# Grouped-query attention: keys and values of all tokens first, query finishes among the attention units, output products in halves, three engines in source order

## The chip, the cores and the metric

The kernel runs as one program on one core of a Trainium2 chip. The metric is the device time of one execution in microseconds (us). The core has TensorE (matmul; PE in the profile, its weight loads PEld), VectorE (DVE), ScalarE (ACT), GpSimd (POOL) and SyncE (SP, which here issues the DMAs). They run beside each other and wait for one another through semaphores; each works through its own list of instructions in order. Matmul results go to PSUM, which this kernel uses as eight banks of 128 x 512 float32. A *granted clock* below 1 in the profile means that TensorE ran at that share of its full speed.

## The reference, cut to what matters

The program computes a gated linear attention block with a feed-forward, then two further layers on 256 latent and 256 context tokens, 1024 features each: neighbourhood attention and a feed-forward, then grouped-query attention (16 query heads, 4 key and value heads of 64 features) and a last feed-forward. The change touches the grouped-query attention, which only the latent tokens leave (`with_ctx_out` is false there):

```python
def qknorm_gqa_mixer(h_lat, h_ctx, w_qkv, q_gain, k_gain, w_o, ang_row, ang_col, with_ctx_out):
    q, k, v = project_qkv(h_lat, w_qkv, GQA_HEADS, GQA_KV_HEADS)
    qc, kc, vc = project_qkv(h_ctx, w_qkv, GQA_HEADS, GQA_KV_HEADS)
    q = axial_rope(rms_norm_2(q, q_gain), ang_row, ang_col)
    k = axial_rope(rms_norm_2(k, k_gain), ang_row, ang_col)
    kc = rms_norm_2(kc, k_gain)
    k_all = jnp.concatenate([kc, k], axis=1)
    v_all = jnp.concatenate([vc, v], axis=1)
    ...
    def block(q_b):
        s = jnp.einsum('bqhgd,bshd->bhgqs', q_b, k_all).astype(jnp.float32) * scale
        p = jax.nn.softmax(s, axis=-1).astype(v_all.dtype)
        return jnp.einsum('bhgqs,bshd->bqhgd', p, v_all)
    ...
    y_lat = jnp.moveaxis(o, 0, 1).reshape(b, s_len, GQA_HEADS * HEAD_DIM) @ w_o
```

All is float32. The result is added to the latent residual through a gate, and the last feed-forward follows.

## The kernel before

**Split numbers and weight units.** Each float32 operand of a large product is split into a rounded high part and a low remainder, and a product is three matmuls (`mm3`, L170 to L173). The weights come as a stream of units of 128 x 1024 (list `UNITS`). `wnext` (L159) takes the next unit: it issues loads about four units ahead on SP (`w_load`, five raw buffers) and converts units ahead of use (`w_split`): ACT rounds the raw unit to its high part (L154), DVE subtracts for the low part (L155). `cap[0]` says how far ahead is converted: with 3, two units beyond the one in use. Twelve buffers hold six converted units.

**Who orders the work.** A scheduler at build time orders each engine's instructions by its own estimates, with the source order as priority, and assigns buffers. Inside a `manual_schedule` region, the engines named keep the order of the source. Before, no such region covers this part.

**The section, in source order.** Token tiles 0 and 1 are latent, 2 and 3 context; `bT2` holds the inputs, transposed and split, for all four.

1. `kv_pass((2, 3))`: keys and values of the context, 16 steps of three matmuls 512 wide (`mm_h`, one feature block k of one token tile). Its four weight units are kept in `kv_units`.
2. `to_T` (L204 to L230): the latent inputs are transposed (L210, two per block, eight blocks and so eight banks), then scaled and shifted from PSUM (even blocks on DVE, L226; odd ones on ACT, L223), rounded on ACT (L228) and subtracted on DVE (L229).
3. `q_proj(0, aq)`: first half of the queries (heads 0 to 7), both latent tiles, 16 steps; beside it, one step of `back` after each, the context's `kv_finish`: square on ACT, sums and gain on DVE, inverse root on POOL (`inv_root`, L176 to L178), rounding and remainder, and `kv_T`, which transposes the keys on TensorE (L1211), high parts first.
4. `kv_steps` for the latent tiles with the kept units, 16 steps; beside it `q_finish(0, ...)` for both tiles: square, sum, inverse root, rotation (`roped`: product L1139, two half products L1144, sum L1147), rounding (L1256), remainder (L1260), and after an empty step the transposes (L1266, one bank for four heads) with their copies (L1270) to `qst`.
5. `gqa_chain`: second half of the queries, tile 0 (8 steps, beside the latent `kv_finish`), then tile 1 and `q_finish(1, ...)`, then the output product.
6. `staged`: 32 units (`gqa_unit`: 16 heads for tile 0, then for tile 1) in a software pipeline, each unit one stage behind the next: two score matmuls into a bank (L1349, L1350); row maximum on DVE (L1355), a small product on POOL; exponential on ACT (L1358); division on DVE (L1364, for some heads on ACT, L1362); four transposes (L1368); copy on ACT (L1371). After a pair of heads comes `gqa_pv`, the product with the values (L1378, 16 matmuls 64 columns wide) and its split copy. `qfill(n)` runs three steps of `gqa_chain` per unit in the first sixteen, one per unit after. The output product takes a weight unit k per step with `mm_r` (six matmuls) as soon as `og_done` has its pair of heads. For tile 0 the units k = 4 to 7 are kept in `held`, so that tile 1 can use them at the end. After each product of tile 1, one step of `attn_out(0)` goes on with the residual and norm of tile 0; then its transposes to `eT`.
7. The held products of tile 1, its gate and norm, and the last feed-forward (`tok_up`).

Of the kernel before, what the change touches and what calls it, by code (L numbers as in the profile page):

```python
# [19 lines left out]
KD = D // P  # L20
# [63 lines left out]
def net(ctx, tc, x, xt, vecs, gk_w, gk_up, gk_b, g_onorm, wst, final_norm, ctx_in, ctx_t, ada, ada_b, cvec,  # L84
# [25 lines left out]
    def bank(dt=F32):  # L110
        return ps.tile([P, 512], dt, tag="bank", bufs=8, name=nm("b"))
# [26 lines left out]
    cap = [3]  # L138
# [190 lines left out]
    def load_gates(L, v):  # L329

        for ci in range(2):
            for half in range(2):
                if (L, ci, v) in grows:
                    gates[(L, ci, v, half)] = t2([512])
                    bcast_row(gates[(L, ci, v, half)], grows[(L, ci, v)], 512 * half, 512)

    def run(gen, n=1):
        for _ in range(n):
            next(gen, None)
# [84 lines left out]
    for f in range(8):  # L424
        u = wnext(("f", "w_in"))
# [113 lines left out]
    for k in range(KD):  # L539
        u = wnext(("r", "w_in", k))  # L540
# [615 lines left out]
    def kv_steps(ac):  # L1156
        for kp in range(4):
            if 2 in ac:
                kv_units.append(wnext(("h", "gqa_qkv", 2 * kp, D)))
                u = kv_units[-1]  # L1160
            else:
                u = kv_units.pop(0)
            for j in range(2):
                k = 2 * kp + j
                for t in ac:
                    mm_h(ac[t], u, j, bT2[k], t, k == 0, k == KD - 1)
                    yield

    def kv_pass(tiles):
        ac = {t: bank() for t in tiles}  # L1170
        for _ in kv_steps(ac):
            pass
        return ac
# [56 lines left out]
    def q_proj1(ac, t):  # L1230
        for kp in range(4):
            if t == 0:
                q1_units.append(wnext(("h", "gqa_qkv", 2 * kp, 512)))
            for j in range(2):
                k = 2 * kp + j
                mm_h(ac[t], q1_units[kp], j, bT2[k], t, k == 0, k == KD - 1)
                yield
# [35 lines left out]
    def alternate(gens):  # L1273
        while gens:
            for g in list(gens):
                if next(g, "end") == "end":
                    gens.remove(g)
                yield

    def beside(front, back):  # L1280

        for _ in front:
            next(back, None)

    cap[0] = 3
    load_gates(1, 2)
    acx = kv_pass((2, 3))
    to_T(xn, bT2, 0, mod(1, 0, 1), mod(1, 0, 0))
    back = alternate([kv_finish(acx, t) for t in (2, 3)])
    aq = [bank(), bank()]  # L1290
    beside(q_proj(0, aq), back)
    run(back, 100)
    aq0 = [aq[0], t2([512])]
    A.copy(out=aq0[1], in_=aq[1])
    back = alternate([q_finish(0, aq0, t) for t in range(2)])
    acl = {t: bank() for t in (0, 1)}
    beside(kv_steps(acl), back)
    run(back, 100)
    back = alternate([kv_finish(acl, t) for t in range(2)])
    aq = [bank(), bank()]  # L1300

    def gqa_chain():

        yield from q_proj1(aq, 0)
        yield from alternate([q_proj1(aq, 1), q_finish(1, aq, 0)])
        q1_units.clear()
        yield from q_finish(1, aq, 1)
        for t, k in [(0, k) for k in range(KD)] + [(1, k) for k in range(KD // 2)]:
            if k == 0:
                oacc.append([bank() for _ in range(2)])  # L1310
            while (k, t) not in og_done:
                yield
            u = wnext(("r", "gqa_o", k))
            if k >= KD // 2:
                held.append((k, u))
            mm_r(oacc[t], u, og[k], t, k == 0, k == KD - 1)
            if t == 1:
                run(out0)
            yield
        run(out0, 9)  # L1320
        yield
        yield from to_T_steps([xn[0]], eT, 0, mod(1, 0, 4), mod(1, 0, 3))

    def attn_out(t):
# [9 lines left out]
    oacc, og_done, held = [], set(), []  # L1334
    out0 = attn_out(0)
    eT = new_T()
    chain_ = gqa_chain()
    for _ in range(11):
        run(chain_)
        run(back, 2)  # L1340
    run(back, 100)

    og = [None] * KD

# [28 lines left out]
    def gqa_pv(hp, t):  # L1373
        po = bank()
        kvh = hp // 2
        for c in range(4):
            for e in range(2):
                T.matmul(po[e * 64:(e + 1) * 64, 0:P], lhsT=vg[(c + 2) % 4][:, kvh * 64:(kvh + 1) * 64],  # L1378
                         rhs=probs[2 * hp + e][:, c, :], start=(c == 0), stop=(c == 3))
        del probs[2 * hp], probs[2 * hp + 1]  # L1380
        yield
        if t == 0:
            z = t2([2, S], F32R)
            og[hp] = (z[:, 0, :], z[:, 1, :])
        o = [z[:, t * P:(t + 1) * P] for z in og[hp]]
        A.copy(out=o[0], in_=po[:, 0:P])
        V.tensor_tensor(out=o[1], in0=po[:, 0:P], in1=o[0], op=ALU.subtract)  # L1387
        og_done.add((hp, t))

    gorder = [(h, t) for t in range(2) for h in range(16)]  # L1390

    def qfill(n):
        run(chain_, 3 if n < 16 else 1)

    def qdone(m):
        head, t = gorder[m]
# [1 line left out]

    xn = []
    staged([lambda z=z: gqa_unit(*z) for z in gorder], qfill, qdone)  # L1400
    run(chain_, 200)
    for ks in (held[:-1], held[-1:]):
        for hf in range(2):
            c = slice(hf * 512, (hf + 1) * 512)
# [2 lines left out]
            if k == KD - 1:  # L1407
                gated(lat[1], oacc[1][hf], 1, 0, 2, hf)
    xn.append(normed(lat[1]))


    load_gates(1, 5)
# [178 lines left out]
```

## Time and profile before

| | us |
|---|---|
| median of 3 runs | 1278.57 |
| lowest, highest | 1278.46, 1279.03 |
| the profiled execution, its own time | 1278.93 |
| its span | 1277.1 |
| PE busy in the span | 1251.0 (98%) |
| DVE busy | 926.6 (73%) |
| ACT busy | 684.9 (54%) |
| POOL busy | 74.7 (6%) |

Busy time is the time in which at least one instruction of the engine is shown. A matmul's row lasts longer than the distance to the next one's start, since matmuls overlap; so the work of a stretch is read from distances between starts, and idle time from rows that name what ended it (`[0.45 <-ACT t L1201]`: idle 0.45 us, ended by ACT's instruction of line 1201). A group's row in the table of groups holds line, engine, operation, output and input with their shapes, the count, then busy us and mean ns, then the idle time before.

### The profile page before, as it was taken

How to read it: one execution, taken by the hardware profiler on the slowest of the kernel's cores; microseconds unless marked ns; L12 is line 12 of the kernel's file. 1: busy time of each engine (PE TensorE's matmuls, PEld its weight loads, DVE VectorE, ACT ScalarE, POOL GpSimd, SP SyncE). 2: the span in 40 equal slices, each digit the busy share in tenths (PEclk: the TensorE clock that was granted, in tenths of full speed). 3: DMA queues.
4: the chain of work that ended last, by engine and by line, in shares of the span. 5: the costliest groups of instructions: out<-in, count | busy, mean ns of one | idle time of the engine just before them, and what ended most of it. 6: DMA issues, size and time to landing. Idle time of an engine off the chain costs nothing.

```text
span 1277.1 us, 18786 instructions
## 1 busy us (share of the span) xinstructions
PE 1251.0 (98%) x6969; PEld 1048.0 (82%) x6969; DVE 926.6 (73%) x1640; ACT 684.9 (54%) x1305; POOL 74.7 (6%) x131
## 2 busy tenths in 40 slices
PE   7999999999999999999999999999999899999997
PEld 6888889988788877789888888888887677899996
DVE  4878788797988888777877777533668887655554
ACT  6565655666548888754232122233457877644443
POOL 1000000030100000001000000000002210000000
PEclk9999999999999999999999999999999999999999
DMA  9526587887573333463656778624654234666650
GB/s 342 182 93 213 184 294 250 286 269 257 182 253 96 115 115 119 155 199 114 213 177 212 245 263 267 192 85 120 204 171 133 60 86 128 200 188 184 186 176 34
DMA packets 68796, 231.23 MB, mean 181 GB/s; under 512 B 8208, under 2 KB 9152, under 8 KB 68704
## 3 DMA queue, kind: packets, MB, share of 16 engines
q1 hardware_dynamic: 68416, 229.94, 56.1%
q8 instruction: 55, 0.90, 0.3%
q14 instruction: 37, 0.30, 0.1%
q10 hardware_dynamic: 288, 0.09, 0.0%
HBM read 228.93 MB, written 1.07 MB: 180 GB/s over the span
## 4 chain that ended last, share of the span: by engine, by line
PE 83%; DVE 8%; ACT 6%; issue 1%; DMA 1%; POOL 0%; ACTq 0%; POOLq 0%; DVEq 0%
PE b L171 25%; PE b L172 25%; PE b L173 25%; DVE wl L155 2%; PE b L1378 1%; ACT wh L154 1%; PE b L1368 1%; PE b L503 1%; PE b L210 1%; DVE a L300 1%; DVE t L300 1%; PE b L1349 1%; ACT t L854 1%; PE b L1350 0%; PE b L933 0%
## 5 line engine op out<-in xcount | busy, mean ns | idle before, releaser
L154 ACT CAST wh<-raw 128x1024 fp32r<-128x1024 f32 x310 | 322.3, 1043 | 408.2 <-PE b L172 310.6
L155 DVE TENSOR_TENSOR wl<-raw,wh 128x1024 fp32r<-128x1024 f32 x310 | 375.6, 1218 | 161.3 <-ACT wh L154 158.0
L172 PE MATMUL b<-t,wl 128*128 128x256 f32 (+1 forms) x1120 | 366.4, 327 | 0.4 <-DVE wl L155 0.4
L171 PE MATMUL b<-t,wh 128*128 128x256 f32 (+1 forms) x1120 | 366.8, 328 | 0.0
L173 PE MATMUL b<-t,wh 128*128 128x256 f32 (+1 forms) x1120 | 365.8, 327 | 0.0
L171 PE MATMUL b<-wh,t 128*128 128x512 f32 (+1 forms) x747 | 297.4, 401 | 0.5 <-ACT t L682 0.3
L172 PE MATMUL b<-wh,t 128*128 128x512 f32 (+1 forms) x747 | 295.3, 395 | 0.4 <-DVE t L610 0.2
L173 PE MATMUL b<-wl,t 128*128 128x512 f32 (+1 forms) x747 | 294.9, 395 | 0.0
L172 PEld LDWEIGHTS b<-t,wl 128*128 128x128 f32 x1120 | 211.3, 189 | 22.8 <-DVE wl L155 0.7
L171 PEld LDWEIGHTS b<-t,wh 128*128 128x128 f32 x1120 | 211.2, 189 | 22.6 <-ACT wh L154 0.3
L173 PEld LDWEIGHTS b<-t,wh 128*128 128x128 f32 x1120 | 211.0, 189 | 20.6 <-DVE t L229 0.2
L173 PEld LDWEIGHTS b<-wl,t 128*128 128x128 f32 x747 | 140.3, 188 | 33.7
L172 PEld LDWEIGHTS b<-wh,t 128*128 128x128 f32 x747 | 140.7, 188 | 32.9 <-DVE t L1387 1.5
L171 PEld LDWEIGHTS b<-wh,t 128*128 128x128 f32 x747 | 140.2, 188 | 31.7 <-ACT t L682 0.9
L300 DVE CUSTOM_DVE_ANT_0 a<-a,crow 128x1024 f32<-128x1024 f32 x96 | 117.7, 1233 | 27.7 <-DMA a<-in_ada_dram 27.4
L300 DVE CUSTOM_DVE_ANT_0 t<-a,crow 128x1024 bf16<-128x1024 f32 x64 | 78.0, 1228 | 7.3 <-DMA a<-in_ada_dram 7.2
L1041 DVE TENSOR_TENSOR t<-b,t 128x512 f32<-128x512 f32 (+1 forms) x42 | 23.7, 563 | 61.6 <-PE b L173 54.5
L183 POOL TENSOR_TENSOR c<-c,mhalf 128x1 f32<-128x1 f32 x21 | 14.2, 674 | 539.0 <-DVE c L182 538.9
L315 POOL TENSOR_TENSOR mod<-mod,bcol 128x8 f32<-128x8 f32 x20 | 15.2, 759 | 477.5 <-DVE mod L300 475.2
L1047 ACT CAST t<-t 128x512 fp32r<-128x512 f32 (+1 forms) x42 | 21.7, 517 | 23.2 <-DVE t L1041 23.1
L190 ACT ACTIVATE t<-t 128x512 f32<-128x512 f32 x40 | 24.8, 624 | 9.1 <-DVE t L1010 4.7
L1358 ACT ACTIVATE t<-b,c,c 128x512 f32<-128x512 f32 x32 | 25.2, 790 | 0.3 <-POOL c L1356 0.2
(225 smaller groups left out, 1198.5 us busy)
## 6 DMA issues: line engine op xcount, KB each, us to landing
raw<-in_wst_dram SPq DMA_DIRECT2D x310, 512.0 KB, 4.3
a<-in_ada_dram SPq DMA_DIRECT2D x96, 512.0 KB, 4.4
t<-in_rpb_dram SPq DMA_DIRECT2D x16, 256.0 KB, 4.6
t<-row SPq DMA_DIRECT2D x12, 256.0 KB, 4.6
t<-in_ctx_dram SPq DMA_DIRECT2D x8, 256.0 KB, 6.1
t<-in_xt_dram SPq DMA_DIRECT2D x4, 256.0 KB, 4.0
t<-in_x_dram SPq DMA_DIRECT2D x4, 256.0 KB
crow<-in_cvec_dram SPq DMA_DIRECT2D x2, 512.0 KB
```

Source lines behind the costliest of these rows:

```text
L154: A.copy(out=h[:, :n], in_=raw[:, :n])
L155: V.tensor_tensor(out=l[:, :n], in0=raw[:, :n], in1=h[:, :n], op=ALU.subtract)
L171: T.matmul(o, lhsT=lh, rhs=rh, start=first, stop=False)
L172: T.matmul(o, lhsT=ll, rhs=rh, start=False, stop=False)
L173: T.matmul(o, lhsT=lh, rhs=rl, start=False, stop=last)
L183: G.tensor_tensor(out=ms[:, 3:4], in0=ms[:, 2:3], in1=mhalf[:, 0:1], op=ALU.pow)
L190: A.activation(out=junk[hf], in_=halves[hf], func=AF.Square, scale=1.0 / 32.0, accum_out=ms[:, hf:hf + 1])
L300: V.tensor_tensor_reduce(out=raw if ci == n_c - 1 else t2([D], BF16), in0=raw, in1=crow[ci], scale=1.0, scalar=0.0, op0=ALU.mult, op1=ALU.add,
L315: G.tensor_tensor(out=m, in0=m, in1=bcol[:, L, v, :], op=ALU.add)
L1041: V.tensor_tensor(out=a, in0=pg_[:, :n], in1=a, op=ALU.mult)
L1047: A.copy(out=h, in_=a)
L1358: A.activation(out=pl, in_=sl, func=AF.Exp, scale=r, bias=mx[:, 1:2], accum_out=mx[:, 2:3])
```

## The change

Only the grouped-query section changes. (1) From the context's `kv_pass` to the norm of the last latent tile, PE, ACT and DVE keep source order; SP and POOL stay with the scheduler, and so does the place of work from outside the region. (2) The latent keys and values come directly behind `to_T`, with the context's `kv_finish` beside them; the first query half comes after, with the latent `kv_finish` beside it. (3) Tile 0 of the first half is finished beside ten steps of the second half (eight for tile 0, two for tile 1); the other three `q_finish` run inside the units, two steps per unit in the first sixteen and one after, and the six steps left of the second half run one per unit. (4) The output product runs one half of the columns per unit (`mm_h`, three matmuls), and `og_done` is set one step later. (5) From k = 6 of the output product the conversion runs one unit ahead (`cap[0] = 2`), until the region ends.

```diff
     cap[0] = 3
     load_gates(1, 2)
+    in_order = tc.manual_schedule(engines={mybir.EngineType.PE, mybir.EngineType.Activation, mybir.EngineType.DVE})
+    in_order.__enter__()
     acx = kv_pass((2, 3))
     to_T(xn, bT2, 0, mod(1, 0, 1), mod(1, 0, 0))
     back = alternate([kv_finish(acx, t) for t in (2, 3)])
+    acl = {t: bank() for t in (0, 1)}
+    beside(kv_steps(acl), back)
+    run(back, 100)
+    back = alternate([kv_finish(acl, t) for t in range(2)])
     aq = [bank(), bank()]
     beside(q_proj(0, aq), back)
     run(back, 100)
     aq0 = [aq[0], t2([512])]
     A.copy(out=aq0[1], in_=aq[1])
-    back = alternate([q_finish(0, aq0, t) for t in range(2)])
-    acl = {t: bank() for t in (0, 1)}
-    beside(kv_steps(acl), back)
+    aq = [bank(), bank()]
+    back = q_finish(0, aq0, 0)
+    projs = [q_proj1(aq, t) for t in range(2)]
+    for n in range(10):
+        run(projs[n // 8])
+        if n < 9:
+            run(back)
     run(back, 100)
-    back = alternate([kv_finish(acl, t) for t in range(2)])
-    aq = [bank(), bank()]
-
-    def gqa_chain():
-
-        yield from q_proj1(aq, 0)
-        yield from alternate([q_proj1(aq, 1), q_finish(1, aq, 0)])
+
+    def finishes():
+
+        yield from q_finish(1, aq, 0)
+        yield from q_finish(0, aq0, 1)
+        run(projs[1], 9)
         q1_units.clear()
         yield from q_finish(1, aq, 1)
+
+    def oproj():
+
         for t, k in [(0, k) for k in range(KD)] + [(1, k) for k in range(KD // 2)]:
             if k == 0:
                 oacc.append([bank() for _ in range(2)])
             while (k, t) not in og_done:
                 yield
+            if k == KD - 2:
+                cap[0] = 2
             u = wnext(("r", "gqa_o", k))
             if k >= KD // 2:
                 held.append((k, u))
-            mm_r(oacc[t], u, og[k], t, k == 0, k == KD - 1)
-            if t == 1:
-                run(out0)
-            yield
+            for hf in range(2):
+                mm_h(oacc[t][hf], u, hf, og[k], t, k == 0, k == KD - 1)
+                if t == 1:
+                    run(out0)
+                yield
         run(out0, 9)
-        yield
         yield from to_T_steps([xn[0]], eT, 0, mod(1, 0, 4), mod(1, 0, 3))
...
-    chain_ = gqa_chain()
-    for _ in range(11):
-        run(chain_)
-        run(back, 2)
-    run(back, 100)
+    finish_, oproj_ = finishes(), oproj()
...
         V.tensor_tensor(out=o[1], in0=po[:, 0:P], in1=o[0], op=ALU.subtract)
+        yield
         og_done.add((hp, t))
...
     def qfill(n):
-        run(chain_, 3 if n < 16 else 1)
+        if n < 6:
+            run(projs[1])
+        run(finish_, 2 if n < 16 else 1)
+        run(oproj_)
...
-    run(chain_, 200)
+    run(oproj_, 200)
...
     xn.append(normed(lat[1]))
+    in_order.__exit__(None, None, None)
+    cap[0] = 3
```

## The prediction, made before the change was run

> **What bounds the kernel now.** I read the page's chain that ended last first, then a table of stretches, then TensorE's own order of time where the table shows it idle.
>
> ```profile
> PE 83%; DVE 8%; ACT 6%; issue 1%; DMA 1%; POOL 0%; ACTq 0%; POOLq 0%; DVEq 0%
> ```
>
> TensorE carries the chain; DMA is 1% of it. So what counts is time in which TensorE has no matmul of the changed section. The section runs from about 957 to 1085 us:
>
> ```profile
> 957.67:970.72 13.05, 13.05 (x68) 10.21 (x66) 10.29 (x24) 10.69 (x28) 3.02 (x4) 1.00 0.36 94
> 970.72:983.29 12.57, 12.57 (x66) 10.34 (x66) 12.28 (x26) 8.36 (x17) 3.96 (x4) 1.00 0.36 108
> 983.29:991.30 8.01, 7.43 (x42) 5.85 (x42) 5.85 (x18) 5.56 (x19) 2.58 (x4) 1.00 0.58 207
> 991.30:1010.20 18.90, 15.77 (x85) 12.40 (x84) 17.05 (x42) 15.24 (x33) 7.28 (x12) 0.91 0.18 55
> 1010.20:1028.85 18.65, 18.64 (x144) 14.36 (x142) 15.05 (x31) 17.67 (x37) 2.40 (x7) 1.00 0.35 94
> 1028.85:1056.02 27.17, 27.17 (x209) 21.64 (x208) 22.31 (x48) 21.15 (x49) 2.28 (x12) 1.00 0.25 73
> 1056.02:1085.23 29.21, 28.45 (x187) 20.87 (x186) 22.03 (x53) 21.38 (x51) 2.42 (x7) 1.00 0.44 133
> ```
>
> Columns: stretch, length, busy us (count) of PE, PEld, DVE, ACT, POOL, then granted clock. In order: first queries (q0); keys and values of the latent tokens; first half of the second queries (q1); start of attention; token tile 0; tile 1; the tail. Only the third, fourth and last have idle PE, and only the fourth a clock under 1. In it the softmax of the first heads is late:
>
> ```profile
> 1004.54 0.43 PE L1378 MATMUL b<-t,t 128*64 128x128 f32 x2 [1.05 <-ACT t L1371]
> ...
> 1006.74 1.97 PE L1378 MATMUL b<-t,t 128*64 128x128 f32 x14 [1.10 <-ACT t L1371]
> ```
>
> TensorE waits 1.05 and 1.10 us for ACT's copies of transposed probabilities. The value product (L1378) is split 2+14: the scheduler put two matmuls ahead and something else between. Then the clock:
>
> ```profile
> 1003.11:1006.53 3.42, 1.48 (x8) 0.64 (x6) 3.42 (x9) 3.42 (x8) 2.38 (x3) 1.00 0.47 153
> 1006.53:1009.94 3.41, 3.20 (x19) 2.82 (x20) 2.96 (x9) 2.28 (x7) 0.68 (x3) 0.50 0.00 0
> ```
>
> After a stretch in which PE was busy 1.48 of 3.42 us, it ran 3.41 us at half clock: 1.7 us of full-speed work lost.
>
> The first, the seventeenth and the nineteenth score:
>
> ```profile
> 992.78 0.39 PE L1349 MATMUL b<-t,t 128*128 128x512 f32 x1
> ...
> 1028.85 0.47 PE L1349 MATMUL b<-t,t 128*128 128x512 f32 x1
> ...
> 1033.27 0.47 PE L1349 MATMUL b<-t,t 128*128 128x512 f32 x1
> ```
>
> The last two are a steady pair of heads, 4.42 us apart. That is all TensorE: the stretch 1028.85 to 1056.02 is 27.17 of 27.17 busy.
>
> **The change, part by part.** No matmul is added or removed. A step of a projection is three 512-wide matmuls; these start 0.24 apart, 0.7 us a step:
>
> ```profile
> 988.51 0.40 PE L172 MATMUL b<-wh,t 128*128 128x512 f32 x1
> 988.75 0.39 PE L173 MATMUL b<-wl,t 128*128 128x512 f32 x1
> 989.27 0.53 PE L1211 MATMUL b<-identr,t 128*128 128x128 f32 x4
> 990.25 1.22 PE L1211 MATMUL b<-identr,t 128*128 128x128 f32 x12 [0.45 <-ACT t L1201]
> ```
>
> (The last two rows are the latent key transposes, 0.0875 us each when they flow, 12 from 990.25 to 991.30; 16 took 2.03, so an old stall of 0.6, which moves away.) What changes is order, and that on PE, ACT and DVE each instruction now waits behind all that the source puts ahead of it. I follow the source; prices:
>
> ```profile
> L155 DVE TENSOR_TENSOR wl<-raw,wh 128x1024 fp32r<-128x1024 f32 x27 | 32.8, 1220 | 8.0 <-ACT wh L154 7.0 <-PE b L173 0.8
> L1355 DVE TENSOR_REDUCE c<-b 128x1 f32<-128x512 f32 x32 | 21.9, 687 | 2.6 <-PE b L1350 2.1
> L1260 DVE TENSOR_TENSOR t<-t,t 128x256 fp32r<-128x256 f32 x8 | 2.9, 419 | 0.0
> L1147 DVE TENSOR_TENSOR t<-t,t 128x512 f32<-128x512 f32 x4 | 2.6, 680 | 0.0
> L154 ACT CAST wh<-raw 128x1024 fp32r<-128x1024 f32 x27 | 28.3, 1053 | 8.2 <-PE b L172 7.6 <-ACT t L1358 0.3
> L1371 ACT COPY t<-b 128x512 f32<-128x512 f32 x32 | 18.8, 589 | 3.4 <-PE b L1368 3.2
> L1256 ACT CAST t<-t 128x256 fp32r<-128x256 f32 x8 | 2.8, 414 | 4.7 <-DVE t L1147 4.7
> L178 POOL TENSOR_TENSOR c<-c,mhalf 128x4 f32<-128x4 f32 x4 | 4.2, 1054 | 0.3
> ```
>
> *A. Latent inputs in source order (to_T), then keys and values.* Before, the scheduler let the first-step operations of later blocks run ahead:
>
> ```profile
> 956.00 1.91 PE L210 MATMUL b<-cm,t 128*128 128x128 f32 x16
> 956.42 0.99 DVE L226 TENSOR_SCALAR t<-b,mod,mod 128x256 f32<-128x256 f32 x2 [0.79 <-PE b L210]
> 956.64 0.57 ACT L223 ACTIVATE t<-b,mod,mod 128x256 f32<-128x256 f32 x1 [3.12 <-PE b L210]
> 957.10 1.01 ACT L228 CAST t<-t 128x256 fp32r<-128x256 f32 x3
> 957.67 0.48 PE L171 MATMUL b<-wh,t 128*128 128x512 f32 x1
> ```
>
> In source order the even block's cast (ACT, 957.10) comes before the odd block's activation (0.57, to 957.97), then its cast (0.4), then DVE's subtraction, and only behind that the next even block on DVE: 2.36 us for two blocks (956.42 to about 958.78) and the last cast at 965.4. Two costs. First, six of eight banks are free for the eight transposes; the new accumulators wait for the third block's read, ending 959.3: PE starts at 959.4 instead of 957.67, +1.7, less the 0.4 by which the first stretch's 13.05 us exceed 48 matmuls of 0.233 and 16 key transposes: **+1.3**. Second, the context keys' finish now stands on ACT behind all that: square 965.4, reduction and gain on DVE, two inverse roots one after the other on POOL (1.05 each, with an add ahead) until about 969.2, casts of 0.41, a subtraction queued behind the second tile's product, a last cast to 970.8. PE reaches the first key transposes after 11 of 16 steps, 959.7 + 11 x 0.7 = 967.4, and cannot pass them: high halves wait to 969.2, low halves from 969.5 to 970.9, **+3.2** (ends 0, were the chain as early as before, and 3.5).
>
> ```profile
> raw<-in_wst_dram SPq DMA_DIRECT2D x310, 512.0 KB, 4.3
> ```
>
> The weight loads on SP belong to the same calls and move with them; a landing of 4.3 us against a lead of four units (eight steps at least, 5.6 us) keeps them off the path.
>
> *B. First query finish beside q1.* Before, it lay beside the latent keys, which convert no weights. Now it has 27 matmuls, 6.3 us, of cover, and the same ten steps convert four weight units. DVE: 4 x 1.22 + reduction 0.69 (as L1355) + product 0.68 + two halves 0.84 + sum 0.68 + two subtractions 0.84 = 8.6. Besides, its first conversion waits for ACT (a bank copy and a cast, about 2 us), and the last cast on ACT stands behind the query's two casts, which wait for the sum: about 1.9 us in which DVE has nothing, less 1.2 for overlapped ends. So the subtractions end near 11.3, and PE waits **5.0** (ends 2.0, without the ACT waits, and 6). Against it go 0.6 of the old key stall and 0.7 of eight transposes done later: **+3.7** net. A and B: the first score comes about 8 us later.
>
> *C. Units of token tile 0.* From the first score (992.8) to the seventeenth (1028.85), 36.1 us before. Now three query finishes spread over them, and there is no projection to fill units 6 to 8, since the output product starts at unit 9 (the extra yield delays it by one). Per pair, the steady stretch gives DVE 22.31/27.17 x 4.42 = 3.6 and ACT 3.4. A query finish (five units) adds on DVE 0.68 x 3 + 0.42 x 4 = 3.7, so 1.5 a pair: 5.1 for DVE against 4.7 for PE. All three now turn in step: the value product waits for a copy that ACT queues last, ACT's copies for transposes, DVE's reductions behind a conversion. At DVE's rate 16 units take 40.8, +4.7; with each wait counted in full I walk to 44, +8; nothing is lost if the engines run ahead. I take **+4**.
>
> *D. Tile 1 and tail.* No finishes any more; halves give each unit one 0.7 us filler where before every second unit had 1.4. The splits go:
>
> ```profile
> 1057.95 0.43 PE L1378 MATMUL b<-t,t 128*64 128x128 f32 x2
> 1058.31 0.50 PE L1349 MATMUL b<-t,t 128*128 128x512 f32 x1
> 1058.65 0.40 PE L1350 MATMUL b<-t,t 128*128 128x512 f32 x1
> 1059.12 1.09 PE L1378 MATMUL b<-t,t 128*64 128x128 f32 x14
> ```
>
> One costs about 0.6 (the detour 0.36, the gap 0.2); four or five of them and the idle 0.76 of the last stretch are **-3** (ends -5, and 0 if the held products, now behind the units, leave the last softmax uncovered). The lower cap leaves one unit converted ahead: 2.3 us of work against 4.42 a pair, free.
>
> *Clock.* A stall of 5 us holds a stretch of 3.41 us less busy than the 1.48 that cost the half clock before. The old one (1.7) goes, one or two come, partly where PE waits anyway: **+1** (0 to 3.4). [...]
>
> Sum: 4.5 + 3.7 + 4 - 3 + 1 = +10.2. The profiled execution took 1278.93 (its span is 1277.1), 0.4 above the median of 1278.57. Predicted: **1289.1 us**, slower.
>
> **Rivals.**
> *The order pays (faster).* From 957.67 to 1085.23 PE spent 127.6 us; by counts it needs 264 wide matmuls (144 in the three projections, 96 output products, 24 of the next stage) x 0.233 = 61.5, 16 pairs x 3.0 = 48 (4.42 less a product of 1.4), 6.5 for other transposes: 116. If ACT and DVE run ahead so that A's and B's transposes find their data, half of the 11.6 us goes: 1273.1. For it: ACT is busy 10.69 of 13.05 and 8.36 of 12.57 us where these finishes lie, so there is room. Against: room does not help an engine whose next instruction waits. It turns on two points: last key cast before 967.4, first query's subtractions within 6.3 us of q0's end. Chance 0.25.
> *No change.* Early loss and late gain cancel, or the order is nearly what the scheduler had made (its steady stretch is full): 1278.9. Chance 0.09.
> *Lockstep in full.* C at +8, clock +2, D at 0: +18, 1297. It is the upper end of slower, 0.1 of the 0.66.
>
> **Chances and range.** A measurement here tells about 0.2%, 2.6 us. Slower by more 0.66, within 0.09, faster 0.25. The slower case alone spans 1281.4 (A 2.5, B 1, C 1, D -3, clock 1) to 1297; the range takes in half of the faster case and leaves out under 0.2: 1273 to 1297.
>
> **What would show it.** Right: PE waits of over 1 us ahead of context key transposes and ahead of the first query transposes; half clock shortly behind; fewer heads a microsecond up to the seventeenth score; value products always 16 in a row; steady pairs of 4.4 in tile 1. Wrong: both transposes start without a wait, or the seventeenth score comes within 37 us of the first.

## The result and the profile after

| | before | after |
|---|---|---|
| median, us | 1278.57 | 1308.25 |
| lowest, highest | 1278.41, 1279.82 | 1306.74, 1308.61 |
| the profiled execution, its span | 1278.93, 1277.1 | 1308.61, 1306.8 |

The changed kernel is **slower by 29.7 us**: ratio 1.0228, with a 95% interval from 1.0217 to 1.024 (five executions of each). The direction was forecast, the size was not: 1308.25 lies 11 us above the upper end of the range. The profiled execution is the longest of the five, 0.4 us above the median.

First the page's chain, by engine:

```profile
PE 80%; DVE 9%; ACT 8%; issue 2%; POOL 1%; DMA 1%; ACTq 0%; POOLq 0%; DVEq 0%
```

TensorE's share fell from 83 to 80%, and ACT's and DVE's rose. The transfers keep their 1%. Where TensorE was without work shows in the table of stretches. The columns are those of the prediction: stretch, length, busy us (count) of PE, PEld, DVE, ACT, POOL, granted clock, DMA share, GB/s.

```profile
957.24:968.12 10.88, 8.63 (x36) 6.24 (x35) 6.27 (x16) 6.24 (x17) 2.35 (x4) 1.00 0.01 2
968.12:975.90 7.78, 6.35 (x26) 5.24 (x27) 4.18 (x12) 3.69 (x13) 0.40 (x1) 0.57 0.00 0
...
989.81:1003.68 13.87, 9.34 (x41) 6.84 (x40) 8.73 (x15) 6.69 (x13) 2.74 (x2) 0.87 0.52 163
...
1014.18:1029.78 15.60, 11.53 (x71) 8.17 (x69) 8.94 (x21) 10.04 (x25) 2.90 (x6) 0.78 0.00 1
1029.78:1049.69 19.91, 17.32 (x113) 12.78 (x111) 13.71 (x31) 14.24 (x32) 3.17 (x8) 0.91 0.27 80
...
1086.64:1101.61 14.97, 10.13 (x86) 7.46 (x85) 8.51 (x22) 8.52 (x22) 0.38 (x2) 1.00 0.23 70
```

In order: latent keys and values up to the first context key transposes; those transposes and the matmuls behind them; the second query half with the first finish; the second and third part of units 1 to 16, which run from the first score (1003.68) to the seventeenth (1049.69); the drain behind the last score. Before, only one stretch had idle TensorE worth a microsecond. Now each of these has, and in the drain it is idle for 4.84 of 14.97 us at full clock. In four of them the granted clock is below 1; before, in one.

What TensorE waited for, from the view of its waits between 955 and 1120 us (in total, times, longest):

```profile
PE b L1388 <- ACT t L1381: 8.1, 7, 2.3
PE b L1266 <- DVE t L1260: 4.5, 1, 4.5
PE b L1378 <- DVE t L1374: 3.1, 2, 1.9
PE b L1211 <- ACT t L1201: 1.4, 1, 1.4
```

Line numbers of the attention unit moved by ten: scores L1359, maximum L1365, exponential L1368, division L1374 (on ACT L1372), transposes L1378, copy L1381, value product L1388. The longest entry is one that the prediction named without a price of its own: the value product waits for ACT's copies of the probabilities, 8.1 us in seven places. Before, nothing in this section cost more than 2.5 us in total.

The stages of all kernels that follow, from TensorE's rows of each trace. "To first score" is counted from the first transpose of the latent inputs (`to_T`), which came between 954.9 and 957.0 us in these executions; that scatter is there already at 535 us, in work that is the same in all. "Half clock" sums the stretches between 955 us and the end of the section whose granted clock was 0.50; "next" is the first transpose of the last feed-forward's token projection:

| kernel | to first score | 1st to 17th score | 17th to 32nd | 32nd to next | half clock |
|---|---|---|---|---|---|
| before | 36.8 | 36.1 | 35.2 | 28.5 | 3.4 |
| **after** | 48.1 | 46.0 | 37.0 | 34.7 | 23.9 |
| e1 no region | 35.9 | 42.2 | 34.0 | 29.4 | 6.8 |
| e2 old order, region | 49.8 | 36.3 | 48.2 | 38.6 | 23.9 |
| e3 ACT and DVE ordered | 42.5 | 42.7 | 36.6 | 37.9 | 17.1 |
| e4 PE ordered | 36.1 | 39.9 | 33.7 | 32.4 | 3.4 |
| e5 PE kept busy | 44.6 | 44.4 | 37.0 | 34.7 | 0 |
| e6 inputs one pair ahead | 41.7 | 46.1 | 37.0 | 34.7 | 17.1 |
| e7 value product later | 46.5 | 42.1 | 35.8 | 33.7 | 10.2 |
| e8 halves only | 36.8 | 36.2 | 33.7 | 27.7 | 3.4 |
| e9 drain free | 45.6 | 46.0 | 37.1 | 32.0 | 17.1 |
| e10 query finish first | 45.7 | 46.0 | 37.0 | 34.7 | 17.1 |
| e11 all four mends | 40.6 | 42.7 | 35.8 | 29.4 | 10.2 |
| e12 halves, early table | 36.8 | 35.1 | 33.7 | 27.7 | 3.4 |

After against before: +11.3, +9.9, +1.8 and +6.2 us, together 29.2 of the 29.7. Each stage is one profiled execution, and the half clock differs between executions of one kernel (mean clocks of 0.988 to 0.993 in the five of after), so a stage is known less well than a median. The stages hold nearly the same matmuls in both kernels; the largest difference is behind the last score (the drain), where six wide matmuls more stand after the change (78 against 72), 1.4 of the 6.2 us.

One execution of e4 took 2489.16 us at a mean clock of 1.0, for a reason that stays open; e4's median is over its other three.

### The profile page after: what moved, and what is told of

The parts are those of the page before. It is cut to its first block, busy times and chain, and to the rows that moved or that the text cites. A ratio compares the mean times of both kernels' runs of the same rounds, so it can differ in the third digit from the quotient of the medians.

```text
span 1306.8 us, 18799 instructions
## 1 busy us (share of the span) xinstructions
PE 1263.3 (97%) x6969; PEld 1055.9 (81%) x6969; DVE 927.1 (71%) x1640; ACT 684.3 (52%) x1305; POOL 74.7 (6%) x131
## 4 chain that ended last, share of the span: by engine, by line
PE 80%; DVE 9%; ACT 8%; issue 2%; POOL 1%; DMA 1%; ACTq 0%; POOLq 0%; DVEq 0%
PE b L171 24%; PE b L172 24%; PE b L173 24%; DVE wl L155 2%; ACT wh L154 1%; PE b L1388 1%; PE b L503 1%; PE b L210 1%; ACT t L1368 1%; DVE a L300 1%; DVE t L300 1%; ACT t L854 1%; ACT t L1381 0%; PE b L933 0%; ACT t L876 0%
## 5 line engine op out<-in xcount | busy, mean ns | idle before, releaser
L173 PEld LDWEIGHTS b<-t,wh 128*128 128x128 f32 x1120 | 211.2, 189 | 20.6 <-DVE t L229 0.2
L1388 PE MATMUL b<-t,t 128*64 128x128 f32 x256 | 23.3, 290 | 8.1 <-ACT t L1381 8.1
```

The lines of the kernel that those rows point to most:

```text
L173: T.matmul(o, lhsT=lh, rhs=rl, start=False, stop=last)
```

## The experiments

Ratios are to the kernel before on the same chip, whose median was 1278.6 each time; each has its 95% interval, about 0.0015 to either side (1.9 us). So two kernels of this list are told apart by some 2 to 3 us, not by less.

### The new order without the region, and the region without the new order

e1 removes the region from the changed kernel:

```diff
-    in_order = tc.manual_schedule(engines={mybir.EngineType.PE, mybir.EngineType.Activation, mybir.EngineType.DVE})
-    in_order.__enter__()
     acx = kv_pass((2, 3))
...
-    in_order.__exit__(None, None, None)
```

> The changed kernel without the source-order region: the new order of the source only as the scheduler's priority. If the loss of 29.7 us comes from keeping source order (waits that nothing may pass, and the half clock behind them): 1275 to 1283 us. If it comes from the moved work itself (latent keys first, finishes among the units, halves): 1295 us or more.

e2 puts the same three lines into the kernel before, and nothing else of the change.

> The kernel before with only the region added (PE, ACT, DVE in source order; nothing moved). If source order costs: at least 1290 us, with PE waits at other places (the wide products of the chain run out in the first sixteen units). If moved work costs: within 4 us of 1278.6.

Measured: **e1 1284.72 us**, ratio 1.0046 (1.0031 to 1.0061); **e2 1314.98 us**, ratio 1.030 (1.0273 to 1.0327). The moved work costs 6.1 us by itself when the scheduler orders the engines; the region costs 36.4 us on the old order and 23.5 us on the new one. So source order is the larger cause, on whichever order it is laid, and the new order is in fact the better of the two for it. e1 lies 1.7 us above the lower of its two expected ranges, so both causes are there. In e1 the first score comes as early as before, and all of the loss lies in units 1 to 16, where the three query finishes now stand (42.2 us against 36.1). Stage by stage, the region adds 12.2 us ahead of the first score of the new order, 3.8 in units 1 to 16 and 8.3 behind them (after less e1).

TensorE's longest waits in e1, then in e2:

```profile
PE b L1386 <- ACT t L1379: 3.6, 2, 2.9
```

```profile
PE b L1380 <- ACT t L1373: 12.2, 10, 2.6
...
PE b L1370 <- DVE t L1009: 2.8, 1, 2.8
```

In e2 the value product (there L1380) waits ten times for its copies, and at two places TensorE waits (2.8 and 2.4 us) for a bank that the gate of token tile 0 (L1009) has still to read; that read stands on DVE behind a conversion. That is the same kind of wait as after the change, in other places.

### Which engines the order binds

e3 names only ACT and DVE in the region, e4 only PE:

```diff
-    in_order = tc.manual_schedule(engines={mybir.EngineType.PE, mybir.EngineType.Activation, mybir.EngineType.DVE})
+    in_order = tc.manual_schedule(engines={mybir.EngineType.Activation, mybir.EngineType.DVE})
```

> The changed kernel with ACT and DVE in source order and PE left to the scheduler. If late results of ACT and DVE are the cause, PE has little to put in their place: 1295 us or more. If PE's own fixed order is the cause, about 1283 us.

```diff
+    in_order = tc.manual_schedule(engines={mybir.EngineType.PE})
```

> The changed kernel with PE alone in source order, ACT and DVE left to the scheduler. If late results of ACT and DVE (to_T in lockstep, conversions ahead of the query finish) are the cause: about 1285 us, without the 1.3 us wait at the context keys. If PE's fixed order is: 1297 us or more.

Measured: **e3 1300.35 us**, ratio 1.0172 (1.0156 to 1.0187); **e4 1285.05 us** (median of three), ratio 1.0057 (1.0039 to 1.0075). Over e1, the order on ACT and DVE costs 15.6 us and that on PE alone nothing that these intervals tell from zero; all three together cost 23.5, about 8 more than the two singly. That fits one reading, which these two runs suggest and don't prove: late results come from ACT and DVE, and a free PE fills part of the holes with other matmuls.

### Is it the clock?

Between the waits TensorE ran at half clock: 0.50 by the profile. Its wide matmuls started 0.426 us apart there (six between 1004.23 and 1006.36 us) and 0.233 apart at full clock (thirteen between 961.26 and 964.06), which makes 0.55 of full speed. The stretch ahead of the first of these episodes and the episode itself, then the start of the one at 1017 us:

```profile
965.80:969.22 3.42, 1.76 (x10) 1.04 (x8) 1.71 (x5) 0.92 (x3) 2.53 (x3) 1.00 0.00 0
969.22:972.63 3.41, 2.54 (x12) 2.15 (x13) 1.41 (x6) 1.78 (x8) 0.00 (x0) 0.50 0.00 0
972.63:976.05 3.42, 3.42 (x12) 2.82 (x12) 2.11 (x5) 1.71 (x5) 0.00 (x0) 0.50 0.00 0
...
1013.60:1017.02 3.42, 1.51 (x9) 0.96 (x9) 2.23 (x5) 2.36 (x6) 1.41 (x2) 1.00 0.00 0
1017.02:1020.43 3.41, 2.31 (x16) 1.58 (x16) 3.34 (x10) 2.03 (x6) 1.16 (x4) 0.50 0.00 0
```

Behind a stretch busy for 1.76 of 3.42 us (51%) the clock was down for 6.8 us: TensorE still had a wait in the first half of the episode (2.54 of 3.41 us busy), and the clock came back behind a half that was full (3.42 of 3.42 us). e5 puts 47 matmuls whose results nobody reads into six of the waits of the changed kernel, into a bank of their own or one that is written over next:

```diff
+    def busy(o, w, n):
+
+        for _ in range(n):
+            T.matmul(o, lhsT=w[:, 0:P], rhs=w, start=True, stop=True)
...
+            if t == 2:
+                busy(bank(), bT2[0][0], 4 if dst is kHs else 5)
...
+        if (hf, t) == (0, 0):
+            busy(bank(), bT2[0][0], 17)
...
+        if (head, t) == (2, 0):
+            busy(pt, kHs[0], 7)
...
+        if t == 0 and hp in (0, 3):
+            busy(po, kHs[0], 9 if hp else 5)
```

> The changed kernel with 47 extra 512-wide matmuls whose results nobody reads, placed on PE where it waits: 4 and 5 ahead of the first context key transposes, 17 ahead of the first query transposes, 7 ahead of the transposes of unit 2, 5 and 9 ahead of two value products. At full clock they take 11 us, all inside waits. If the half clock is a large part of the loss: three of the four half-clock stretches go and the time falls by 5 to 10 us (1298 to 1303) although PE does more. If the waits alone are the loss: 1308 to 1314 us.

Measured: **1305.21 us**, ratio 1.0208 (1.019 to 1.0225). The episodes are gone, as the same places show in e5:

```profile
965.80:969.20 3.40, 3.40 (x15) 2.44 (x13) 2.17 (x6) 1.77 (x7) 2.15 (x4) 1.00 0.00 0
969.20:976.10 6.90, 6.51 (x38) 5.20 (x38) 4.30 (x13) 4.45 (x16) 0.61 (x1) 1.00 0.00 0
```

Yet only 3.0 us came back, less than expected. At 0.233 a matmul the 47 take 11.0 us; the idle gaps over 0.25 us in the section fell from 21.5 to 13.9 us, so 7.6 of it filled waits and some 3.4 delayed real work. So the clock by itself is worth about 6.4 us, an estimate. The five executions of the changed kernel point lower: the three at a mean clock of 0.988 or 0.989 took 1.5 us more than the two at 0.993, and at that rate, again an estimate, the 23.9 us at half clock are worth about 3. By rows it looks like more: the seven stretches at half clock hold 20.6 us of busy time, so 10.3 us of full-speed work was lost at the granted 0.50, against 1.6 before; at the 0.55 of the distances between starts it was some 9.3. The difference is work that would have waited anyway. The clock follows from the waits and is not the main cause: with no half clock left in the section, e5 is still 26.7 us slower than the kernel before.

### The three places, one at a time

e6 changes `to_T` so that the first step of a later pair of blocks comes ahead of the rounding of the pair before, on each engine:

```diff
+            rs.append(t2([n]))
+            if k % 2:
+                A.activation(out=rs[k], in_=pt[:, :n], func=AF.Identity, scale=scale[:, k:k + 1],
+                             bias=bias[:, k:k + 1])
+            else:
+                V.tensor_scalar(out=rs[k], in0=pt[:, :n], scalar1=scale[:, k:k + 1], scalar2=bias[:, k:k + 1],
+                                op0=ALU.mult, op1=ALU.add)
+            if k >= 2:
+                split(k - 2)
...
-    to_T(xn, bT2, 0, mod(1, 0, 1), mod(1, 0, 0))
+    to_T_ahead(xn, bT2, 0, mod(1, 0, 1), mod(1, 0, 0))
```

> The changed kernel with the source of to_T for the latent inputs written so that each block's first step stands two blocks ahead of its rounding; all else kept in source order. By step A of the prediction: accumulators start about 1.1 us earlier, the context key transposes wait under 1 us instead of 2.9, the half clock at 969 us goes: 1300 to 1303 us. If A is not on the path that sets the end: 1307 us or more.

Measured: **1303.06 us**, ratio 1.019 (1.0175 to 1.0205), 5.2 less than after. TensorE's rows after, at the new accumulators and at the context key transposes, then the same in e6:

```profile
958.84 0.50 PE L171 MATMUL b<-wh,t 128*128 128x512 f32 x1 [0.92 <-DVE t L226]
...
968.12 0.54 PE L1211 MATMUL b<-identr,t 128*128 128x128 f32 x4 [1.10 <-ACT t L1198]
970.09 0.75 PE L1211 MATMUL b<-identr,t 128*128 128x128 f32 x4 [1.42 <-ACT t L1201]
```

```profile
958.13 0.48 PE L171 MATMUL b<-wh,t 128*128 128x512 f32 x1
...
967.09 0.53 PE L1237 MATMUL b<-identr,t 128*128 128x128 f32 x4 [0.59 <-ACT t L1227]
```

3.44 us of waits became 0.59, and the half clock behind them went too; the first score comes 6.4 us earlier by the table of stages.

e7 lets the value product take its place one step later, behind the next unit's work, with `og_done` set at the same step as in the changed kernel:

```diff
     def gqa_pv(hp, t):
+        yield
         po = bank()
...
-        yield
         og_done.add((hp, t))
```

> The changed kernel with each value product one unit later (the empty step stands ahead of it instead of behind its copy). If the waits of the value products for ACT's copies (8.1 us in 7 places) are a cause of their own: 1300 to 1304 us. If ACT and DVE are simply behind, the wait moves to the output product or the transposes: 1306 us or more.

Measured: **1300.42 us**, ratio 1.0171 (1.0156 to 1.0187), 7.8 less, as expected. This is the largest gain of the edits that leave the region in place. What made the product wait is read in ACT's order of time after the change, around the longest of these waits, with TensorE's rows of the same moment:

```profile
1037.20 0.43 PE L1388 MATMUL b<-t,t 128*64 128x128 f32 x2
1039.94 1.09 PE L1388 MATMUL b<-t,t 128*64 128x128 f32 x14 [2.31 <-ACT t L1381]
```

```profile
1037.33 0.71 ACT L1256 CAST t<-t 128x256 fp32r<-128x256 f32 x2 [1.84 <-DVE t L1147]
1037.94 0.77 ACT L1368 ACTIVATE t<-b,c,c 128x512 f32<-128x512 f32 x1
...
1038.71 0.71 ACT L1372 ACTIVATE t<-t,c 128x512 f32<-128x512 f32 x1
1039.32 0.57 ACT L1381 COPY t<-b 128x512 f32<-128x512 f32 x1
```

The first head's copy is there, so two matmuls start; the other fourteen need the second head's, which stands on ACT behind the exponential and the division of younger units, and behind a query finish's cast that itself waited 1.84 us for DVE. With the product one step later the copy is done by then, and e7's waits for it come to 0.9 us in one place, where they were 8.1 in seven.

Yet the other half of the expectation holds in part too: waits moved. In e7's trace TensorE waits 4.6 us for DVE's divisions, where it was 3.1, and at new places for 0.7 to 1.4 us each; its idle gaps over 0.25 us in the section come to 21.3 us, against 21.5 after. What became less in that trace is the time at half clock (10.2 us against 23.9). That the gain is not the clock alone is seen in the one execution of e7 with a mean clock of 0.989: 1302.79 us, against 1308.25 of the changed kernel at 0.989. How the 7.8 us divide between the wait and what followed from it is not shown.

e9 closes the region at the last score, so that the drain is left to the scheduler:

```diff
     def qfill(n):
+        if n == 32:
+            in_order.__exit__(None, None, None)
```

> The changed kernel with the region left at unit 32, when the last scores are out: the softmax of the last heads, the held products and the last norm go back to the scheduler. If the tail's loss (from the 32nd score to the next stage 6 us more than before) comes from source order: 1302 to 1304 us. If it comes from halves or the held products: 1307 us or more.

Measured: **1303.61 us**, ratio 1.0193 (1.0177 to 1.0209), 4.6 less, as expected in total. By the stages, 2.7 us lie in the drain (34.7 to 32.0), and 2.5 ahead of the first score, where no edit was made: the profiled execution of after had the 6.8 us episode at 969 and this one had none. So the drain's own order is worth nearer 3 than 5, and part of the 4.6 may be chance.

e10 turns the two engines' work beside the second query half around: the finish's step first, then the projection's step with its conversion:

```diff
     for n in range(10):
-        run(projs[n // 8])
         if n < 9:
             run(back)
+        run(projs[n // 8])
```

> The changed kernel with each step of the first query finish written ahead of the projection step (and so of its weight conversion), instead of behind it. By step B: the subtractions no longer stand behind the fourth conversion, the wait ahead of the first query transposes falls from 4.5 to about 2.2 us: 1305 to 1306.5 us. If that wait is made up later anyway: 1308 us.

Measured: **1306.37 us**, ratio 1.0212 (1.0198 to 1.0226). That is 1.9 less, within what was expected, but its interval overlaps that of the changed kernel, so the gain is not shown. The rows show a trade. After, ahead of the first query transposes, then e10:

```profile
1001.28 0.72 PE L1266 MATMUL b<-identr,t 128*128 128x128 f32 x4 [4.47 <-DVE t L1260]
```

```profile
995.84 0.50 PE L173 MATMUL b<-wl,t 128*128 128x512 f32 x1 [0.66 <-DVE wl L155]
...
998.80 0.72 PE L1266 MATMUL b<-identr,t 128*128 128x128 f32 x4 [1.75 <-DVE t L1260]
```

2.7 us of the wait went, and TensorE waits for converted weights instead. The two chains compete for the same engines; their order moves the wait.

### All four mends, and the halves alone

e11 makes the edits of e6, e7, e9 and e10 together in the changed kernel.

> The changed kernel, still in source order to unit 32, with four edits at once: first steps of to_T ahead, query finish ahead of the conversion, value product one unit later, tail left to the scheduler. If the causes add: 1308.3 - 5.2 (to_T) - 7.8 (value product) - 2.3 - 5 = 1288 us, still slower than before. If they share one cover, such as the half clock: 1293 us or more.

Measured: **1290.18 us**, ratio 1.009 (1.0076 to 1.0104), 18.1 less than after. The four alone gave 5.2 + 7.8 + 4.6 + 1.9 = 19.5: they add up nearly in full, 2 us over what was expected for that case, so no mend covers another by much, and together they hold 18 of the 29.7 us. It is still 11.5 over before, of which 3.8 lies ahead of the first score (40.6 against 36.8) and 6.6 in units 1 to 16 (42.7 against 36.1), where e1, with no region, loses 6.1.

e8 puts only the output product's halves into the kernel before:

```diff
-            mm_r(oacc[t], u, og[k], t, k == 0, k == KD - 1)
-            if t == 1:
-                run(out0)
-            yield
+            for hf in range(2):
+                mm_h(oacc[t][hf], u, hf, og[k], t, k == 0, k == KD - 1)
+                if t == 1:
+                    run(out0)
+                yield
```

> The kernel before with the output product in halves and nothing else. If halves are harmless or good: 1276 to 1280 us. If they carry the 6 us that the new order costs without a region: about 1284 us.

Measured: **1276.49 us** (ten executions, 1275.10 to 1277.27), ratio 0.9983 (0.9973 to 0.9992): 2.1 us faster than before. Up to the seventeenth score it stands as before, and it gains 1.5 in units 17 to 32 and 0.8 behind them, where the halves do their work (three wide matmuls, 0.7 us, went from the former to the latter). So this part of the change is good, and the moved work (e1 less e8) costs about 8 us.

Among the waits that e8 keeps from before is one of about 1 us ahead of the first transposes of probabilities, behind ACT's load of the table for the exponential (1.28 us at 996.38 us before). e12 adds one small exponential to e8, whose result nobody reads, ahead of the section's latent keys:

```diff
     A.copy(out=aq0[1], in_=aq[1])
+    A.activation(out=col()[:, 0:8], in_=mhalf, func=AF.Exp)
```

> The kernel before with the output product in halves and one small exponential, read by nobody, written ahead of the attention, so that ACT loads its table for the exponential there. If the first exponential's table load (1.28 us at 996.4 us before) and the half clock behind that ramp are on the path: 1273.5 to 1275.5 us. If not: 1276.5 us as with halves alone.

Measured: **1275.85 us** (eleven executions, 1274.54 to 1277.45), ratio 0.9977 (0.9968 to 0.9986). The wait, as the kernel before has it:

```profile
1000.75 0.63 PE L1368 MATMUL b<-cm,t 128*128 128x128 f32 x4 [0.98 <-DVE c L1360]
```

In e12 these transposes start at 1000.56 with no wait. The load moved (in e12 it takes 1.28 us at 965.61) without a cost that the trace shows: the first score comes 36.8 us behind the first transpose, as in e8, and units 1 to 16 take 1.1 us less (35.1 against 36.2). But the median is only 0.6 us below that of e8, within the intervals, so a gain is not shown. e12 and e8 are the fastest versions, about 0.2% faster than the kernel before.

## Why the prediction was wrong, and where it was right

The sum failed above all at D: -3 was forecast for token tile 1 and the tail, and +8.0 came, 11 of the 19 us by which the time was missed. C was about half of what came, and the clock was put low; A and B held. The stages set beside the steps:

| step | predicted | as measured | clock taken out by rows | in e5, without half clock |
|---|---|---|---|---|
| A and B, to the first score | +8.2 | +11.3 | +7.1 | +7.8 |
| C, units 1 to 16 | +4 | +9.9 | +5.4 | +8.3 |
| D, the rest | -3 | +8.0 | +8.0 | +8.0 |
| clock | +1 | in the rows above | +8.7 | none |

The fourth column takes out half the busy time of the stretches at half clock (4.2 us ahead of the first score, 6.1 in units 1 to 16 where before had 1.6). That is the most that the clock can have cost. The last column holds e5's extra matmuls, part of which delayed real work.

**A: right in mechanism and place, somewhat high in size.** The cycle of two blocks was forecast at 2.36 us; DVE's rows start 955.99 and 958.25:

```profile
955.99 0.54 DVE L226 TENSOR_SCALAR t<-b,mod,mod 128x256 f32<-128x256 f32 x1 [0.79 <-PE b L210]
...
958.25 0.54 DVE L226 TENSOR_SCALAR t<-b,mod,mod 128x256 f32<-128x256 f32 x1
```

That is 2.26. The waits fell at the three places named: 0.92 ahead of the accumulators, 1.10 and 1.42 ahead of the keys' high and low halves, 3.4 us where 4.5 were forecast. e6 removed all but 0.59. What was missed is the 6.8 us at half clock right behind.

**B: right.** Forecast: the query's subtractions end about 11.3 us after the first query half, and PE waits 5.0. Measured: the query half ends at 989.81, the transposes start at 1001.28, 11.5 later, after a wait of 4.47. DVE's and ACT's rows show the step named, each engine waiting for the other in its fixed order:

```profile
996.04 1.21 DVE L155 TENSOR_TENSOR wl<-raw,wh 128x1024 fp32r<-128x1024 f32 x1
997.17 0.68 DVE L1147 TENSOR_TENSOR t<-t,t 128x512 f32<-128x512 f32 x1
999.57 1.23 DVE L155 TENSOR_TENSOR wl<-raw,wh 128x1024 fp32r<-128x1024 f32 x1 [1.72 <-ACT wh L154]
1000.72 0.76 DVE L1260 TENSOR_TENSOR t<-t,t 128x256 fp32r<-128x256 f32 x2
```

```profile
997.89 0.71 ACT L1256 CAST t<-t 128x256 fp32r<-128x256 f32 x2 [3.63 <-DVE t L1147]
998.50 1.04 ACT L154 CAST wh<-raw 128x1024 fp32r<-128x1024 f32 x1
```

ACT stands 3.63 us at the cast for DVE's sum; only then comes ACT's last conversion, for which DVE stands 1.72 us ahead of the subtraction. The prediction gave "about 1.9 us in which DVE has nothing".

**C: right in mechanism, half the size.** The value of +4 went by DVE's rate; the walk with "each wait counted in full" gave +8. Measured it is +9.9, and +8.3 in e5 without any half clock (with 21 of its extra matmuls, 4.9 us, in the stage). After, e9 and e10 have the same order in these units; they lost 6.1, 4.4 and 4.6 us to the half clock by rows and took 46.0 us each, since what the clock cost less, TensorE waited more (6.9, 8.3 and 8.2 us idle). That points to the waits as what set the stage's length, and to the choice of DVE's rate over the walk as the step at fault. ACT's groups of the stretch from the first to the seventeenth score show the lockstep (busy us, mean ns, idle before, releaser):

```profile
L1270 ACT CAST t<-b 128x512 fp32r<-128x512 f32 x7 | 4.1, 593 | 6.3 <-PE b L1266 6.3
...
L1256 ACT CAST t<-t 128x256 fp32r<-128x256 f32 x6 | 2.1, 402 | 5.5 <-DVE t L1147 5.5
```

In 46.0 us ACT stood 11.8 us at instructions of the query finishes (L1256, L1270), with copies that TensorE waited for queued behind some of them. But the region isn't all of C: e1 loses 6.1 in this stage without it, so spreading the finishes over the units costs about as much on free engines.

**D: the step that failed, by 11 us and in its sign.** The prediction priced the removed splits at "-3 (ends -5, and 0 ...)": one costs 0.6, and they go. But the splits had been the scheduler's way round a late copy. The copy behind the split that the prediction shows at 1057.95 and 1059.12, in ACT's order before:

```profile
1058.49 0.58 ACT L1371 COPY t<-b 128x512 f32<-128x512 f32 x1
```

It ended at 1059.07, and the fourteen matmuls started then. Without the detour TensorE stands at the same place, between the second and the third matmul: six of the sixteen value products after the change stand there, two in units 1 to 16 (one of them at 1037.20 and 1039.94, as shown), one in units 17 to 32 (the first row below) and three in the drain. Nowhere did the working ask when the second head's copy is ready in ACT's fixed order. In the middle of tile 1 it is ready, and pairs of heads take 4.42 to 4.53 us, near the forecast; but the first pair takes 6.05 us, with the wait of this row, and the last two 5.38 and 4.75, where e8 takes 4.42 for each:

```profile
1053.10 1.09 PE L1388 MATMUL b<-t,t 128*64 128x128 f32 x14 [1.07 <-ACT t L1381]
...
1069.20 0.48 PE L1359 MATMUL b<-t,t 128*128 128x512 f32 x1
...
1073.62 0.48 PE L1359 MATMUL b<-t,t 128*128 128x512 f32 x1
```

Most of the loss lies in the drain, where no later unit's work fills TensorE and the norm and the inputs of tile 0 (L226, L228) share the same engines. TensorE's longest wait there in the view of its waits, before and after, and rows of after:

```profile
PE b L1378 <- ACT t L1371: 0.4, 2, 0.2
...
PE b L1388 <- ACT t L1381: 3.6, 4, 1.3
```

```profile
1091.40 1.09 PE L1388 MATMUL b<-t,t 128*64 128x128 f32 x14 [1.29 <-ACT t L1381]
...
1094.50 0.65 PE L1378 MATMUL b<-cm,t 128*128 128x128 f32 x4 [1.21 <-DVE t L1374]
...
1096.17 1.09 PE L1388 MATMUL b<-t,t 128*64 128x128 f32 x14 [0.65 <-ACT t L1381]
```

The drain was named ("leave the last softmax uncovered"), but its worst end was put at 0; measured, it took 6.2 us more than before, with 6.0 us of listed waits where before had 0.8. e9 and e11 win back 2.7 and 5.3 of that. That the order did it and not the moved work is seen in the stages of D together: -2.3 us with the halves alone (e8), near the forecast -3, and -0.3 with the whole new order but no region (e1).

**Clock: the place right, the size low.** Half clock came behind stretches with waits, two of them busier (1.51 and 1.76 us) than the 1.48 that the prediction went by. "One or two come" were four episodes, and three of them lasted 6.8 us and not 3.4. The prediction counted one stall and one episode; but in these three TensorE waited in the first half too (busy for 2.54, 2.05 and 2.31 of 3.41 us), and in the one of 3.41 us it did not. By the two estimates above the half clock is worth 3 to 6.4 us, less at most 1.6 that it cost before, against +1.

**The rivals.** "The order pays" fell by both of its points: the last key cast ended behind 967.4 (ACT's L1201 released TensorE at 970.09), and the subtractions came 11.5 us after the query half, not within 6.3. "No change" fell with it. "Lockstep in full", 1297, with C at +8, clock +2, D at 0, came nearest to what happened, and its price of C was right; it was given 0.1, and it lacked D's loss. "Right" signs that came: the waits at both transposes, half clock behind each, fewer heads a microsecond. Steady pairs of 4.4 came only in part, and of "value products always 16 in a row" only the order held.

**What stays open.** How much of e11's remaining 11.5 us is the region and how much the moved finishes was not separated further; e1 puts the moved order at 6 to 8. The lower conversion cap was not run alone. The clock's 6.4 us rests on splitting the matmuls of e5 by idle gaps, and the 3 us on five executions.

## What to carry to other kernels

Before source order is imposed on several engines, walk each engine's list at every place where two of them hand work to each other twice: a rounding on one and a subtraction on the other can each be short and still stand in each other's way. A split or a detour in a scheduled trace can be the cover of a late operand; removing it then moves the wait and doesn't save the detour, so ask when that operand is ready in the new order. Price a part of a change by itself where that can be done: here one of them, the halves, was worth 2.1 us alone and was lost under the other 32.

## What the runs showed of the hardware that was not expected

In the section the half clock of the changed kernel lasted 3.41 us once and 6.83 us three times. In the three long episodes TensorE had an idle stretch in the first half (busy for 2.54, 2.05 and 2.31 us); in the short one it was busy throughout. None of the stretches ahead of the four was without work: TensorE was busy in them for 1.76, 0.31, 1.51 and 1.10 us. The second and the last of them, each with the stretch at half clock that followed (columns as above):

```profile
996.50:999.92 3.42, 0.31 (x2) 0.00 (x0) 1.70 (x3) 1.66 (x3) 0.21 (x1) 1.00 0.69 208
999.92:1003.33 3.41, 2.05 (x9) 1.68 (x9) 1.55 (x3) 0.59 (x1) 0.00 (x0) 0.50 0.59 181
...
1037.49:1040.90 3.41, 1.10 (x16) 0.85 (x14) 1.17 (x5) 3.41 (x8) 0.36 (x1) 1.00 0.19 77
1040.90:1044.31 3.41, 3.41 (x12) 2.76 (x11) 3.34 (x8) 1.35 (x4) 0.32 (x2) 0.50 0.33 64
```

TensorE's longest waits that began in the four stretches were 1.42, 4.47, 1.88 and 2.31 us.

In two executions the same waits did not cost the same. In e9 the two waits ahead of the key transposes came as after the change (1.11 and 1.42 us). In both kernels an edge fell within the second, about 0.4 us into it in e9 and 0.55 after the change; so the stretch up to the edge was busy for 1.88 us in e9 and for 1.76 after, and in e9 the clock stayed full behind both stretches:

```profile
966.28:969.69 3.41, 1.88 (x10) 1.15 (x8) 1.70 (x6) 0.84 (x4) 2.60 (x4) 1.00 0.00 0
969.69:973.11 3.42, 2.42 (x18) 2.15 (x19) 1.98 (x9) 2.70 (x13) 0.00 (x0) 1.00 0.00 0
```

The five executions of the changed kernel had a mean clock of 0.988, 0.993, 0.988, 0.989 and 0.993, and the two at 0.993 were the shortest (1307.13 and 1306.74 us).
